# Forgetting heads: gate sums and split values in 4 KB runs, loads ordered a unit earlier, normalisation a unit later

## The chip, the cores and the metric

The kernel runs on one core of a Trainium2 chip. The metric is the device time of one execution in microseconds (us); before the change the median of three runs is 1835.76 us (1833.45 to 1837.6). The engines in the text are TensorE (PE; its weight loads are PEld), VectorE (DVE), ScalarE (ACT), GpSimd (POOL) and SyncE (SP). SP issues all DMAs of this kernel, in order, on one queue that 16 DMA engines serve.

## The reference: what is computed

One layer of a decoder trunk over 1024 tokens of width 1024, in float32. It has a SwiGLU feed-forward half-step, a token mixer of two groups of heads, and a second SwiGLU half-step, each with a residual, a LayerNorm and a modulation by a conditioning vector. The change touches the token mixer:

```
proj = h @ w_in                       # q_a k_a v_a (window heads), q_b k_b v_b (forgetting heads), f_logit
log_f = log_sigmoid(f_logit + b_forget)            # 1024 tokens x 8 heads
cum = cumsum(log_f, axis=tokens)                   # the gate sums
# window group: 8 heads of 64 on 2 key heads, 128-token window, ALiBi, a sink for each head
# forgetting group: 8 heads of 64, causal over all tokens
s[t, j] = q[t] . k[j] / 8 + cum[t] - cum[j]        # j <= t
o = softmax(s) @ v
out = concat(rms_norm(o_a) * gain_a, rms_norm(o_b) * gain_b) @ w_out
```

## The kernel before

All large products work on numbers split into a high and a low part (`split`, lines 101 to 103: ACT rounds to the high part, DVE subtracts to get the low one) and take three products for one (`mm3`), or two where the stacked operand holds both parts. The kernel is written with a tile framework. It takes the program's order as priority, places instructions on each engine by its own estimates of their times, gives a tile a place in its ring when one is free, and sets the waits. What an engine executes is therefore not the program's order exactly, but once placed, each engine and SP's queue go strictly in order. The rings (line 42) have 14 places of 8 KB a partition (h), four of 4 KB in each of z and q, and smaller ones; a ring's name is also a tile's name in the profile.

The token mixer runs from about 660 to 1170 us. First the values of all heads and the forget logits are computed for each of eight token blocks (lines 750 to 772). The high and low parts of the values, 64 + 64 columns a head, are stored to `vd`, whose order is head, token, column (line 763). The gate sums of 128 tokens by 64 (block, head) columns are made by two small products and a chain of small additions (lines 780 to 799), transposed, and stored to `cum_d`, whose order is block, head, token (line 805).

The 13 projections of queries and keys (`proj`) go to `qkd` in DRAM. They are cut into 26 halves that stand in a list of fillers: `fill` (line 925) adds a credit for each piece of attention work and runs the next filler when the credit covers it, and `due(n)` runs fillers until n projections are done. Behind the projections the list has the first half of the output projection.

The window heads come first (`swa_scores`, `swa_values`, `swa_finish` for two groups of eight blocks). Then come the forgetting heads, in four pairs `pr` of two heads `e`. Each head has two units, `q0` = 4 (query blocks 4 to 7) and `q0` = 0 (blocks 0 to 3), so there are 16 units. `fox_scores` (line 1060) makes for a unit four strips, from the last query block to the first: DVE adds the causal mask `cmask` to a 128x128 piece of the head's table `cb` of gate sums (line 1075), PE forms the scores, DVE adds the table to them and takes a running minimum (line 1092), ACT takes the exponential (line 1096). `fox_values` (line 1100) transposes the exponentials on PE, splits them, and multiplies by the split values. `mix` interleaves the values of unit k with the scores of unit k + 1.

`fox_init` (line 1050) issues a head's loads. It is called by strip 7 of the head's first unit. For the first head of a pair it loads the split values of both (`v_load`, h ring), and for each head the query stack, two key stacks, and the table `cb`: the 1024 gate sums of the head, copied to 128 partitions. These four are the z ring's four places for e = 0 and the q ring's for e = 1. `v_load` and the load of `cb` read eight runs of 512 B for each partition.

When a pair's four units are through, `fox_finish` (line 1130) takes the reciprocals of the denominators, transposes them, stores them to `rd` (`recip_rows`, line 863), and calls `normalise` (line 871). That loads them back, copied to 64 partitions for each head, multiplies the outputs, squares the result and adds it to `ssq` for the RMS norm: three DVE operations of 128x1024. The outputs are then stored to `ond`. `swa_finish` does the same with two pairs of a window group.

Of the kernel before, what the change touches and what calls it, by code (L numbers as in the profile page):

```python
# [7 lines left out]
F32 = mybir.dt.float32  # L8
F32R = mybir.dt.float32r
# [37 lines left out]
def layer_kernel(ctx, tc, xT, x, c, adaT, adab, wg1, wu1, wd1, wqk, wv1, wv2, bf, sinks,  # L47
# [29 lines left out]
    def dram(shape, name, dt=F32):  # L77
        return dr.tile(shape, dt, tag=name, name=name, bufs=1)
# [585 lines left out]
    def tok(t):  # L664
        return slice(t * P, (t + 1) * P)
# [61 lines left out]
              steps1)  # L727


    vd = dram([10, S, P], "vd")  # L730
    fz = const([P, NT, NH], "fz")

    def wv_load(src, ncol):
# [16 lines left out]
    for hf in range(2):  # L750
        for pz, (w, ncol) in enumerate(((wva, NV1), (wvb, NV2))):
            for k in range(4):
                t = hf * 4 + k
                p = psum("mm")
                for d in range(KD):
                    hi, lo = h2c(hf, d)
                    mm3(p[:, :ncol], hi[:, k * P:(k + 1) * P], lo[:, k * P:(k + 1) * P],
                        w[d][0], w[d][1], d == 0, d == KD - 1)
                vs = st("w", [P, 5, P], F32R)
                pv = p[:, :5 * HD].rearrange("p (h c) -> p h c", h=5)  # L760
                A.copy(vs[:, :, :HD], pv)
                V.tensor_tensor(vs[:, :, HD:], pv, vs[:, :, :HD].bitcast(F32), ALU.subtract)
                DMA.dma_start(vd[pz * 5:pz * 5 + 5, tok(t), :].rearrange("h t c -> t h c"), vs.bitcast(F32))
                if pz:
                    V.tensor_tensor(fz[:, t], p[:, 5 * HD:NV2], bfb, ALU.add)
                if hf == 0:
                    if t or pz:
                        steps[3 + t + 4 * pz]()
                    if t == 3 and pz:
                        steps[11]()  # L770
                else:
                    park_zn((xa, xb)[pz], pz, k, r1, xpark[0])
# [20 lines left out]
    pc = psum("tp")  # L793
    T.matmul(pc[:, :64], ones, flat(fl), start=True, stop=True)
    V.tensor_copy(flat(fz), pc[:, :64])
    for t in range(1, NT):
        V.tensor_tensor(fw[:, t], fw[:, t], fz[:, t - 1], ALU.add)
        if t + 1 < NT:
            V.tensor_tensor(fz[:, t], fz[:, t], fz[:, t - 1], ALU.add)
    pc = psum("tp")  # L800
    T.transpose(pc[:64, :P], flat(fw), ident)
    cum_sb = st("t", [64, P])
    A.copy(cum_sb, pc[:64, :P])
    cum_d = dram([NT, NH, P], "cum_d")
    DMA.dma_start(cum_d.rearrange("a b c -> (a b) c"), cum_sb)


# [44 lines left out]
        return r  # L852

    def v_load(h0):
        v = st("h", [P, NT, 2, P], F32R)
        for e in range(2):
            DMA.dma_start(v[:, :, e].bitcast(F32), vd[h0 + e].rearrange("(t p) c -> p t c", p=P))
        return v

    rd_d = [dram([n, NT, P], f"rd{i}") for i, n in enumerate((4, 4, 2, 2, 2, 2))]  # L860
# [148 lines left out]
    def swa_values(g, i):  # L1009
        d = swa[g]  # L1010
        sp = d["sp", i // 2][:, i % 2]
        if i == 0:
            d["on"] = st("h", [P, 2, S])
        on = d["on"]
        po = psum("o")
        js = [1] if i == 0 else [0, 1]
        for jj in js:
            pt = psum("tp")
            for hh in range(4):
                T.transpose(pt[:, tok(hh)], sp[:, hh, jj * P:(jj + 1) * P], ident)  # L1020
            ph, pl = st("t", [P, HT], F32R), st("t", [P, HT], F32R)
            split(ph, pl, pt)
            vt = va[:, i - 1 + jj, g]
            T.matmul(po, vt, ph, start=jj == js[0], stop=False)
            T.matmul(po, vt, pl, start=False, stop=jj == 1)
        t = st("t", [P, 2, P])
        pv = po.rearrange("p (b e c) -> p b e c", b=2, e=2)
        for e in range(2):
            own, oth = half_rows(e)
            A.copy(t[own], pv[oth, :, e])  # L1030
            V.tensor_tensor(on[own, :, tok(i)], pv[own, :, e], t[own], ALU.add)
        fill(1.6)

    def swa_finish(g):
        d = swa[g]
        mneg, den, on = d["mneg"], d["den"], d["on"]
        es = small([P, 4, NT], "es")
        for hh in range(4):
            A.activation(es[:, hh], mneg[:, hh], AF.Exp, bias=sinkb[:, 4 * g + hh:4 * g + hh + 1], scale=1.0)
        V.tensor_tensor(den, den, es, ALU.add)  # L1040
        recip_rows(flat(den), 4 * NT, rd_d[g])
        rt = st("h", [P, 2, S])
        for pp in range(2):
            normalise(on[:, pp], rd_d[g][2 * pp:2 * pp + 2], ssq_a, rt[:, pp])
            DMA.dma_start(ond[2 * g + pp], on[:, pp])


    fox = {}
# [1 line left out]
    def fox_init(pr, e):  # L1050
        ring = "zq"[e]
        if e == 0:
            fox[pr] = dict(vp=v_load(2 * pr), den=small([P, 2, NT], "den2"))
        d = fox[pr]
        d["qs", e] = q_stack(5 + pr, e, ring)
        d["ks", e] = k_stack(9 + pr, e, ring)
        cb = d["cb", e] = st(ring, [P, S])
        DMA.dma_start(cb.rearrange("p (a b) -> p a b", a=NT), cum_d[:, 2 * pr + e, :].partition_broadcast(P))

    def fox_scores(pr, e, q0):  # L1060
        def strip(i):
            if i == 7:
                fox_init(pr, e)
            d = fox[pr]
            if i == q0 + 3:
                if q0:
                    sa, sc = st("h", [P, 2, S]), st("h", [P, 2, S])
                    d["sp", e, q0] = {7: sa[:, 0], 6: sa[:, 1], 5: sc[:, 0], 4: sc[:, 1]}
                else:
                    sa = st("h", [P, 4, HT])  # L1070
                    d["sp", e, q0] = {k: sa[:, k] for k in range(4)}
            qs, ks, cb, den = d["qs", e], d["ks", e], d["cb", e], d["den"]


            V.tensor_tensor(cb[:, tok(i)], cb[:, tok(i)], cmask, ALU.add)
            L = (i + 1) * P
            if L <= 512:
                segs = [(0, L)]
            elif L == 640:
                segs = [(0, 384), (384, 256)]  # L1080
            else:
                segs = [(0, 512), (512, L - 512)]
            sp = d["sp", e, q0][i]
            m = None
            for k0, w in segs:
                pp = psum("mm")
                wm = max(w, 256)
                q = qs[:, tok(i)]
                T.matmul(pp[:, :wm], q, ks[0][:, k0:k0 + wm], start=True, stop=False)
                T.matmul(pp[:, :wm], q, ks[1][:, k0:k0 + wm], start=False, stop=True)  # L1090
                mn = small([P, 1], "mneg1", 8)
                V.tensor_tensor_reduce(sp[:, k0:k0 + w], pp[:, :w], cb[:, k0:k0 + w], scale=1.0,
                                       scalar=3e38 if m is None else m, op0=ALU.add, op1=ALU.min,
                                       accum_out=mn)
                m = mn
            A.activation(sp[:, :L], sp[:, :L], AF.Exp, bias=m, scale=-1.0, accum_out=den[:, e, i:i + 1])
            fill(L / 1200)
        return [lambda i=i: strip(i) for i in range(q0 + 3, q0 - 1, -1)]

    def fox_values(pr, e, q0):  # L1100
# [3 lines left out]
        def block(j):  # L1104
# [9 lines left out]
                T.transpose(pt[:, tok(i - q0)], sps[i][:, tok(j)], ident)  # L1114
            ph, pl = st("t", [P, HT], F32R), st("t", [P, HT], F32R)
            split(ph[:, c0:], pl[:, c0:], pt[:, c0:])
            vt = d["vp"][:, j, e]
            T.matmul(po[:, c0:], vt, ph[:, c0:], start=j == 0, stop=False)
            T.matmul(po[:, c0:], vt, pl[:, c0:], start=False, stop=j == q0 + 3)
            if j == q0 + 3:  # L1120
# [9 lines left out]
    def fox_finish(pr):  # L1130
        d = fox[pr]
        on, rt = d["on"][:, 0], d["on"][:, 1]
        recip_rows(flat(d["den"]), 2 * NT, rd_d[2 + pr])
        normalise(on, rd_d[2 + pr], ssq_b, rt)
        if pr < 3:
            DMA.dma_start(ond[4 + pr], on)

    def mix(a, b):

# [14 lines left out]
    for k, (g, i) in enumerate(units):  # L1154
        if k + 1 < len(units):
            if units[k + 1] == (1, 0):
                due(5)
            swa_scores(*units[k + 1])
        swa_values(g, i)
        if i == NT - 1:  # L1160
            swa_finish(g)
    ssq_b = st("b", [P, S])
    G.memset(ssq_b, 0.0)
    filler.append((0.0, lambda: out_init()))
# [4 lines left out]
    credit[0] = 0.0  # L1169
    units = [(pr, e, q0) for pr in range(4) for e in range(2) for q0 in (4, 0)]  # L1170
    due(7)
    for f in fox_scores(*units[0]):
        f()
    for k, u in enumerate(units):
        nxt = []
        if k + 1 < len(units):
            if units[k + 1][1:] == (0, 4):
                due(7 + 2 * units[k + 1][0])
            nxt = fox_scores(*units[k + 1])
        mix(fox_values(*u), nxt)  # L1180
        if u[1:] == (1, 0):
            fox_finish(u[0])
    on_last = fox[3]["on"][:, 0]
    while filler:
        filler.pop(0)[1]()
# [203 lines left out]
```

## Time and profile before

| what | value |
|---|---|
| time of the profiled execution | 1834.09 us |
| its span, first to last instruction | 1832.1 us |
| median of three runs (lowest, highest) | 1835.76 us (1833.45, 1837.6) |
| VectorE busy | 1546.1 us (84%) |
| ScalarE busy | 764.7 us (42%) |
| mean granted TensorE clock | 0.985 |
| moved by DMA | 303.44 MB, 166 GB/s over the span |

The span is the time from the first instruction to the last; the execution's own time has some 2 us around it. An engine's busy time over the span says how much room it has in the mean, and the windows view says it for a stretch. The granted clock is the share of full speed that TensorE was allowed.

### The profile page before, as it was taken

How to read it: one execution, taken by the hardware profiler on the slowest of the kernel's cores; microseconds unless marked ns; L12 is line 12 of the kernel's file. 1: busy time of each engine (PE TensorE's matmuls, PEld its weight loads, DVE VectorE, ACT ScalarE, POOL GpSimd, SP SyncE). 2: the span in 40 equal slices, each digit the busy share in tenths (PEclk: the TensorE clock that was granted, in tenths of full speed). 3: DMA queues.
4: the chain of work that ended last, by engine and by line, in shares of the span. 5: the costliest groups of instructions: out<-in, count | busy, mean ns of one | idle time of the engine just before them, and what ended most of it. 6: DMA issues, size and time to landing. Idle time of an engine off the chain costs nothing.

```text
span 1832.1 us, 23557 instructions
## 1 busy us (share of the span) xinstructions
PE 1755.3 (96%) x8114; PEld 1444.7 (79%) x8114; DVE 1546.1 (84%) x2805; ACT 764.7 (42%) x1465; POOL 23.0 (1%) x32
## 2 busy tenths in 40 slices
PE   7999999999999989999889899999999999999995
PEld 5788888888888879877667777778888888888884
DVE  7999999999597995378678797899788887878999
ACT  5432333233544442277356461543233333344480
POOL 0000000000000000000000000000000000000000
PEclk9999999999999999999989999999999999999998
DMA  9355555558754245855958863333223232675442
GB/s 360 127 197 178 193 193 193 170 173 290 233 167 143 86 134 180 242 148 154 229 143 198 215 205 107 138 109 128 97 99 131 88 108 92 223 231 166 133 144 80
DMA packets 163175, 303.44 MB, mean 166 GB/s; under 512 B 15384, under 2 KB 47728, under 8 KB 163056
## 3 DMA queue, kind: packets, MB, share of 16 engines
q1 hardware_dynamic: 163056, 301.94, 52.1%
q8 instruction: 64, 1.05, 0.2%
q14 instruction: 55, 0.45, 0.1%
HBM read 224.17 MB, written 77.71 MB: 165 GB/s over the span
## 4 chain that ended last, share of the span: by engine, by line
PE 73%; DVE 15%; DMA 6%; ACT 3%; issue 2%; SPq 0%; POOL 0%; DVEq 0%; ACTq 0%; POOLq 0%
PE y L106 10%; PE y L107 10%; PE y L108 10%; PE mm L106 9%; PE mm L108 9%; PE mm L107 9%; PE o L106 3%; PE o L108 3%; PE o L107 3%; DVE w L103 2%; DVE h L103 2%; DMA q<-cum_d 2%; PE tp L107 1%; PE tp L108 1%; PE tp L1114 1%
## 5 line engine op out<-in xcount | busy, mean ns | idle before, releaser
L102 ACT CAST w<-u 128x512 fp32r<-128x512 f32 x303 | 186.6, 622 | 393.1 <-PE y L108 160.2
L106 PE MATMUL y<-h,w 128*128 128x512 f32 x728 | 287.7, 395 | 5.0 <-ACT h L102 2.1
L107 PE MATMUL y<-h,w 128*128 128x512 f32 x728 | 285.6, 392 | 0.0
L108 PE MATMUL y<-h,w 128*128 128x512 f32 x728 | 285.2, 392 | 0.0
L103 DVE TENSOR_TENSOR w<-u,w 128x512 fp32r<-128x512 f32 x303 | 206.5, 686 | 23.4 <-ACT w L102 22.1
L106 PE MATMUL mm<-h,w 128*128 128x512 f32 x528 | 207.7, 394 | 18.7 <-ACT h L102 15.6
L107 PE MATMUL mm<-h,w 128*128 128x512 f32 x528 | 206.7, 392 | 0.3 <-DVE h L103 0.2
L108 PE MATMUL mm<-h,w 128*128 128x512 f32 x528 | 206.7, 392 | 0.0
L106 PEld LDWEIGHTS y<-h,w 128*128 128x128 f32 x728 | 137.5, 189 | 33.5 <-ACT h L102 2.5
L108 PEld LDWEIGHTS y<-h,w 128*128 128x128 f32 x728 | 137.0, 188 | 26.6
L107 PEld LDWEIGHTS y<-h,w 128*128 128x128 f32 x728 | 137.0, 188 | 26.3
L102 ACT CAST w<-t 128x512 fp32r<-128x512 f32 x106 | 65.5, 621 | 185.1 <-PE mm L108 70.3
L106 PEld LDWEIGHTS mm<-h,w 128*128 128x128 f32 x528 | 100.2, 190 | 40.9 <-ACT h L102 16.0
L107 PEld LDWEIGHTS mm<-h,w 128*128 128x128 f32 x528 | 100.0, 189 | 22.2 <-DVE h L103 1.5
L108 PEld LDWEIGHTS mm<-h,w 128*128 128x128 f32 x528 | 99.9, 189 | 21.3 <-DVE w L103 1.0
L102 ACT CAST z<-u 128x512 fp32r<-128x512 f32 x88 | 54.8, 623 | 105.2 <-PE y L108 46.8
L103 DVE TENSOR_TENSOR z<-u,z 128x512 fp32r<-128x512 f32 x88 | 60.5, 689 | 35.7 <-ACT z L102 35.6
L103 DVE TENSOR_TENSOR t<-tp,t 128x512 fp32r<-128x512 f32 (+1 forms) x126 | 72.8, 586 | 18.4 <-ACT t L102 17.7
L102 ACT CAST t<-tp 128x512 fp32r<-128x512 f32 (+1 forms) x126 | 61.8, 502 | 48.3 <-PE tp L1114 47.4
L102 ACT CAST w<-h 128x512 fp32r<-128x512 f32 x111 | 68.2, 617 | 29.4 <-PE o L108 10.5
L103 DVE TENSOR_TENSOR w<-h,w 128x512 fp32r<-128x512 f32 x111 | 75.6, 686 | 1.8 <-ACT w L102 1.8
L103 DVE TENSOR_TENSOR w<-t,w 128x512 fp32r<-128x512 f32 x106 | 72.8, 689 | 1.4 <-ACT w L102 0.8
(356 smaller groups left out, 3948.1 us busy)
## 6 DMA issues: line engine op xcount, KB each, us to landing
u<-aT SPq DMA_DIRECT2D x154, 256.0 KB, 2.7
q<-in_adaT SPq DMA_DIRECT2D x56, 512.0 KB, 3.4
u<-in_wg SPq DMA_DIRECT2D x92, 256.0 KB, 3.0
u<-in_wu SPq DMA_DIRECT2D x90, 256.0 KB, 2.8
aT<-z SPq DMA_DIRECT2D x44, 512.0 KB, 3.2
h<-in_wd SPq DMA_DIRECT2D x88, 256.0 KB, 4.5
qkd<-w SPq DMA_DIRECT2D x26, 512.0 KB, 4.1
aT<-b SPq DMA_DIRECT2D x22, 512.0 KB, 4.2
```

Source lines behind the costliest of these rows:

```text
L102: A.copy(hi, src)
L103: V.tensor_tensor(lo, src, hi.bitcast(F32), ALU.subtract)
L106: T.matmul(o, lh, rh, start=start, stop=False)
L107: T.matmul(o, lh, rl, start=False, stop=False)
L108: T.matmul(o, ll, rh, start=False, stop=stop)
L1114: T.transpose(pt[:, tok(i - q0)], sps[i][:, tok(j)], ident)
```

## The change

Four edits. `vd` is laid out as head, partition, block, column, so that a partition's eight blocks lie together, 4 KB, and the tile of values has the same order. The gate sums are brought into the order head, block before the transposition, by writing the additions to a tile `fo` with a stride, so that `cum_d` is head, block, token and a head's sums are one run of 4 KB. `fox_init` is taken out of strip 7 and called a unit ahead: for the first two heads before the first scores, for every other head at the start of the unit whose scores precede it; the table is loaded before the query stack; `v_load` stays in strip 7. And the loads and the three operations of `normalise`, with the store behind them, are put into a function that is run later: for a window group in block 2 of the next group, or after two strips of the next scores, and for a pair after two strips in the next unit. The last pair's is run after the loop.

```diff
-    vd = dram([10, S, P], "vd")
+    vd = dram([10, P, NT, P], "vd")
...
-                DMA.dma_start(vd[pz * 5:pz * 5 + 5, tok(t), :].rearrange("h t c -> t h c"), vs.bitcast(F32))
+                DMA.dma_start(vd[pz * 5:pz * 5 + 5, :, t, :].rearrange("h p c -> p h c"), vs.bitcast(F32))
...
+    fo = st("t", [P, NH, NT])
+    V.tensor_copy(fo[:, :, 0], fw[:, 0])
     for t in range(1, NT):
-        V.tensor_tensor(fw[:, t], fw[:, t], fz[:, t - 1], ALU.add)
+        V.tensor_tensor(fo[:, :, t], fw[:, t], fz[:, t - 1], ALU.add)
...
-    T.transpose(pc[:64, :P], flat(fw), ident)
+    T.transpose(pc[:64, :P], flat(fo), ident)
...
-    cum_d = dram([NT, NH, P], "cum_d")
+    cum_d = dram([NH, NT, P], "cum_d")
...
-        v = st("h", [P, NT, 2, P], F32R)
+        v = st("h", [P, 2, NT, P], F32R)
         for e in range(2):
-            DMA.dma_start(v[:, :, e].bitcast(F32), vd[h0 + e].rearrange("(t p) c -> p t c", p=P))
+            DMA.dma_start(v[:, e].bitcast(F32), vd[h0 + e])
...
+    later = []
+
     def swa_finish(g):
...
         recip_rows(flat(den), 4 * NT, rd_d[g])
-        rt = st("h", [P, 2, S])
-        for pp in range(2):
-            normalise(on[:, pp], rd_d[g][2 * pp:2 * pp + 2], ssq_a, rt[:, pp])
-            DMA.dma_start(ond[2 * g + pp], on[:, pp])
+
+        def rest():
+            rt = st("h", [P, 2, S])
+            for pp in range(2):
+                normalise(on[:, pp], rd_d[g][2 * pp:2 * pp + 2], ssq_a, rt[:, pp])
+                DMA.dma_start(ond[2 * g + pp], on[:, pp])
+        later.append(rest)
...
         if e == 0:
-            fox[pr] = dict(vp=v_load(2 * pr), den=small([P, 2, NT], "den2"))
+            fox[pr] = dict(den=small([P, 2, NT], "den2"))
         d = fox[pr]
-        d["qs", e] = q_stack(5 + pr, e, ring)
         d["ks", e] = k_stack(9 + pr, e, ring)
         cb = d["cb", e] = st(ring, [P, S])
-        DMA.dma_start(cb.rearrange("p (a b) -> p a b", a=NT), cum_d[:, 2 * pr + e, :].partition_broadcast(P))
+        DMA.dma_start(cb, cum_d[2 * pr + e].rearrange("a b -> (a b)").partition_broadcast(P))
+        d["qs", e] = q_stack(5 + pr, e, ring)
...
         def strip(i):
-            if i == 7:
-                fox_init(pr, e)
             d = fox[pr]
+            if i == 7 and e == 0:
+                d["vp"] = v_load(2 * pr)
...
     def fox_finish(pr):
...
         recip_rows(flat(d["den"]), 2 * NT, rd_d[2 + pr])
-        normalise(on, rd_d[2 + pr], ssq_b, rt)
-        if pr < 3:
-            DMA.dma_start(ond[4 + pr], on)
+
+        def rest():
+            normalise(on, rd_d[2 + pr], ssq_b, rt)
+            if pr < 3:
+                DMA.dma_start(ond[4 + pr], on)
+        later.append(rest)
...
         if i == NT - 1:
             swa_finish(g)
+        elif i == 2:
+            run_all(later)
+            later.clear()
...
     due(7)
+    fox_init(0, 0)
+    fox_init(0, 1)
     for f in fox_scores(*units[0]):
         f()
     for k, u in enumerate(units):
         nxt = []
+        if k and k + 2 < len(units) and units[k + 2][2]:
+            if not units[k + 2][1]:
+                due(7 + 2 * units[k + 2][0])
+            fox_init(*units[k + 2][:2])
         if k + 1 < len(units):
-            if units[k + 1][1:] == (0, 4):
-                due(7 + 2 * units[k + 1][0])
             nxt = fox_scores(*units[k + 1])
+        if later:
+            nxt.insert(2, later.pop())
         mix(fox_values(*u), nxt)
         if u[1:] == (1, 0):
             fox_finish(u[0])
+    run_all(later)
```

## Rows read from the trace of the kernel before

**Rows 1.** The page: busy time of PE; the chain that ended last, by engine.
```profile
PE   1755.3 (96%) x8114; PEld 1444.7 (79%) x8114; DVE 1546.1 (84%) x2805; ACT 764.7 (42%) x1465; POOL 23.0 (1%) x32
PE 73%; DVE 15%; DMA 6%; ACT 3%; issue 2%; SPq 0%; POOL 0%; DVEq 0%; ACTq 0%; POOLq 0%
```

**Rows 2.** Windows: stretch, its us, busy us of each engine, PE's clock, DMA share, GB/s.
```profile
862.00:1040.00 178.00, 157.93 (x796) 126.45 (x795) 129.39 (x326) 93.41 (x208) 2.56 (x1) 0.95 0.75 191
1040.00:1100.00 60.00, 59.25 (x317) 47.13 (x317) 53.53 (x133) 36.87 (x87) 0.00 (x0) 0.98 0.69 207
902.00:905.40 3.40, 3.40 (x14) 2.82 (x13) 2.15 (x7) 1.31 (x4) 0.00 (x0) 0.50 1.05 260
946.40:956.60 10.20, 6.01 (x19) 4.84 (x20) 4.94 (x12) 2.17 (x6) 0.00 (x0) 0.50 0.71 168
...
1038.50:1041.90 3.40, 3.40 (x12) 2.69 (x11) 2.84 (x11) 1.79 (x5) 0.00 (x0) 0.51 1.16 272
```

**Rows 3.** Timeline of DVE: start, us, instruction, in brackets the idle time before it.
```profile
873.93 0.29 DVE L1075 TENSOR_TENSOR z<-z,cmask 128x128 f32<-128x128 f32 x1 [6.05 <-DMA z<-cum_d]
899.92 0.29 DVE L1075 TENSOR_TENSOR q<-q,cmask 128x128 f32<-128x128 f32 x1 [3.65 <-DMA q<-cum_d]
949.64 0.29 DVE L1075 TENSOR_TENSOR q<-q,cmask 128x128 f32<-128x128 f32 x1 [6.62 <-DMA q<-cum_d]
...
965.73 0.68 DVE L1092 CUSTOM_DVE_ANT_0 h<-mm,q 128x512 f32<-128x512 f32 x1
...
977.82 0.29 DVE L1075 TENSOR_TENSOR z<-z,cmask 128x128 f32<-128x128 f32 x1 [1.50 <-DMA z<-cum_d]
997.67 0.29 DVE L1075 TENSOR_TENSOR q<-q,cmask 128x128 f32<-128x128 f32 x1 [3.09 <-DMA q<-cum_d]
1035.97 0.29 DVE L1075 TENSOR_TENSOR z<-z,cmask 128x128 f32<-128x128 f32 x1 [4.80 <-DMA z<-cum_d]
```

**Rows 4.** Timeline of PE: four instructions that ended its longer idle times.
```profile
882.17 0.45 PE L1089 MATMUL mm<-z,z 128*128 128x384 f32 x1 [2.00 <-DVE s_mneg L1092]
901.18 0.50 PE L1089 MATMUL mm<-q,q 128*128 128x512 f32 x1 [3.40 <-DVE s_mneg L1092]
950.59 0.79 PE L1119 MATMUL o<-t,h 128*128 128x512 f32 x1 [6.36 <-DVE t L103]
1036.93 0.39 PE L1089 MATMUL mm<-q,q 128*128 128x256 f32 x1 [3.77 <-DVE s_mneg L1092]
```

**Rows 5.** Timeline of PE and SP near 897; SP's longest waits, 862 to 1040.
```profile
896.76 0.28 PE L1090 MATMUL mm<-z,z 128*128 128x256 f32 x1
...
896.95 0.45 SPq L841 DMA_DIRECT2D z<-qkd  x1
...
SPq L869 <- ACT s_row L868: 18.3, 3, 9.1
```

**Rows 6.** DMA: line 1058's landings; issues, KB of each, median us to landing.
```profile
DMA to landing us min/median/max: 9.0/10.2/10.5
...
h<-in_adaT SPq DMA_DIRECT2D x16, 512.0 KB, 8.5
...
vd<-w SPq DMA_DIRECT2D x16, 320.0 KB, 2.6
h<-vd SPq DMA_DIRECT2D x10, 512.0 KB, 7.2
...
b<-gate_row SPq DMA_DIRECT2D x3, 512.0 KB, 6.8
```

**Rows 7.** Normalisation: DVE's wait, line 875's operations, line 873's landings.
```profile
DVE h L875 <- DMA h<-rd: 2.1, 1, 2.1
...
L875 DVE TENSOR_TENSOR h<-h x4: 1215/1221/1226, 955.3 to 1108.4; 128x1024 f32<-128x1024 f32 x4
...
DMA to landing us min/median/max: 3.6/4.5/11.8
```

More of the change, by code (lines that the diff above doesn't have):

```diff
@@ L1022, in swa_values @@
             split(ph, pl, pt)
-            vt = va[:, i - 1 + jj, g]
+            vt = va[:, g, i - 1 + jj]
             T.matmul(po, vt, ph, start=jj == js[0], stop=False)
@@ L1116, in block @@
             split(ph[:, c0:], pl[:, c0:], pt[:, c0:])
-            vt = d["vp"][:, j, e]
+            vt = d["vp"][:, e, j]
             T.matmul(po[:, c0:], vt, ph[:, c0:], start=j == 0, stop=False)
```

## The prediction

> **What bounds the kernel now.** I read first the page's busy table and chain of waits: TensorE (PE) is busy for 1755.3 of 1832.1 us and holds most of the chain [rows 1], so a change is worth only what it gives PE: idle time, or time at the low clock. The windows view over the stage that the change touches comes next [rows 2]. Of the 178 us from 862 to 1040, in which nearly three of the four pairs of forgetting heads run, PE is idle for 178 - 157.9 = 20.1 us, and its granted clock is 0.95. In the 60 us behind it the same work runs with 0.75 us of idle, while VectorE (DVE) is busy for 53.5 of 60 us: without stalls the stage is PE's, and DVE has just room.
>
> The time-ordered list of DVE shows where the idle time comes from [rows 3]. Six of the eight heads begin with a `cmask` addition (line 1075, strip 7) that finds its table of gate sums (`cb`, loaded from `cum_d`) not landed: 6.05 + 3.65 + 6.62 + 1.50 + 3.09 + 4.80 = 25.7 us. DVE takes its instructions in order, so what stands behind that addition waits too, though it belongs to another unit: the first score reduction of the head whose mask waited until 949.64 starts at 965.73. The addition is put into DVE's order some 16 us before anybody needs it, as soon as the scheduler believes the table to be there. PE then runs out of operands: 3.40, 6.36 and 3.77 us behind three of these waits [rows 4]. Each of the three is followed, or overlapped, by a stretch at clock 0.50 or 0.51, half of full speed (1.2 in place of 2.4 GHz): 902.0 to 905.4, 946.4 to 956.6 and 1038.5 to 1041.9 [rows 2]. PE was busy there for 3.40, 6.01 and 3.40 us; at full clock the same work takes half, so the low clock costs 1.7 + 3.0 + 1.7 = 6.4 us. The other waits (0,0 at 6.05, and 1.50 and 3.09) I price at nothing on PE; under the first one PE had projections to do. Together the masks cost PE 13.5 us idle and 6.4 us slow, 19.9 us.
>
> **The change part by part.** *The order "a unit ahead".* It changes where the loads stand in the program. When they start is another matter: the loads of head (1,0) begin at 896.95, 0.2 us behind the start of the last product on the tiles whose places they take (896.76) [rows 5]. They already go out when a place in the z or q ring comes free, and each head needs all four places of its ring. The new position can't free a place earlier. I take 0 us; at best it saves the time that the table stands behind other issues of SyncE (SP): SP waits 18.3 us in three pieces, at most 9.1 us, for the reciprocal rows (line 869) [rows 5], a wait that the change keeps. At worst it loses nothing by itself, since no head's ring is shared with the unit that is running. `due` forces no projection earlier either: by the credit arithmetic of `fill` the projections that it asks for are done one unit before, in both versions. The table now goes ahead of `qs`; that is two issues of SP, under 1 us of its own.
>
> *Runs of 4 KB.* The table of a head (512 KB: one 4 KB row copied to 128 partitions) is now read as eight runs of 512 B for each partition, and lands 10.2 us after issue (9.0 to 10.5) [rows 6]. Afterwards it is one run of 4 KB for each partition. The trace has a load of just that form: the gate row, 512 KB, one 4 KB row to 128 partitions, median 6.8 us [rows 6]. The bounds: 8.5 us, the slow end among 512 KB loads in 4 KB runs (`adaT`, beside other loads), and 6.8 us. I take 6.8, the same form, so 3.4 us earlier. If DVE comes to each mask when it does now, the waits become 6.05 - 3.4 = 2.65, 0.25, 3.22, 0, 0 and 1.40 us: 7.5 in place of 25.7. On PE the 3.40 goes, 6.36 becomes 3.0 and 3.77 becomes 0.4: 10.1 us less idle. Of the slow stretches I keep one of 3.4 us behind the 3.0 (the idle of 3.40 was followed by one such), 1.7 us, so 4.7 of the 6.4 come back. Sum: -14.8 us. Next late behind the masks are then DVE's ordinary steps, which the stretch 1040 to 1100 shows to be hidden [rows 2].
>
> The Trainium skill, page "DMA: Bandwidth & Descriptors", speaks against this term: its Specifications give 512 B as the least transfer for line rate, and its section "Why small descriptors are slow (HBM only)" counts a fixed 3 cycles for each packet beside one for every 32 B. By that, eight runs of 512 B cost 8 x 19 = 152 cycles against 131 for one of 4 KB, and the table would land after an estimated 10.2 x 131 / 152 = 8.8 us. The gate row's 6.8 us against the table's 10.2 [rows 6] doesn't agree with so small a step, though the two were not loaded beside the same traffic.
>
> *The split values.* Their loads (512 KB in 512 B runs, 7.2 us now) get 4 KB runs too, their stores (2.6 us) keep 512 B runs that then lie 4 KB apart [rows 6]. No stall of the stage falls on either: values are used a unit after the load. Bounds: the loads gain up to 7.2 - 6.8 = 0.4 us by the gate row, or lose 1.3 by the 8.5; the stores could double to 5.2 us, which is what the first window product would come later if nothing lay between. Projections do, so I take 0.
>
> *The gate sums' order.* One more copy of 128x8 and seven additions that write with a stride. A mask addition of 128x128 takes 0.29 us [rows 3], which bounds the copy from above; a stride that doubled the seven would cost 7 x 0.29 = 2.0 at most. I take 0.3 us, on DVE, with PE on projections beside it; it counts in full here.
>
> *The normalisation put off.* Each finish has three operations of 1.22 us on DVE [rows 7], 3.7 us a pair (7.3 for the two pairs of a window group). They are moved by about half a unit, not removed; the reciprocals, their transpose and the write to `rd` stay. What it can gain: the wait of 2.1 us for `h<-rd` [rows 7], and with it the 2.00 us of PE at 882.17 [rows 4]. What it can lose is the last rival's price. It is also one more tile held in the h ring for half a unit. I take 0, between -2.0 and that rival.
>
> Sum: -14.8 + 0.3 = -14.5. The profiled execution took 1834.09 us (1832.1 of span and 2.0 around it), the median of the runs is 1835.76, the lowest 1833.45. 1834.1 - 14.5 = 1819.6; I say **1819.5**.
>
> **Rivals.**
> *All stalls go.* If the schedule gives the tables enough lead, the whole 20.1 us of idle and the 6.4 us of low clock come back: 1834.1 - 26.5 = 1807.6. For it: heads (1,0) and (3,1) have no wait today. Against: the mask is placed by an expected landing, not by need, in all six others.
>
> *The run length is worth half.* A copy of one 4 KB row to 128 partitions may be held back by its source rather than by its runs. With a landing of 8.5 us (1.7 earlier) the waits of 3.65, 6.62 and 4.80 shrink by 1.7 each, PE gets 3 x 1.7 = 5.1 us, and the idle left (1.7, 4.7, 2.1) keeps most of the slow stretches: about 1 us back. 1834.1 - 6.1 = 1828. The skill's estimate of 8.8 us is near this case and would give 1829. For it: the value loads, with the same 512 B runs but no copying, land in 7.2 us. Against: the gate row's 6.8.
>
> *The wait moves along.* If the scheduler's own estimate of the load shrinks with the runs, it puts the mask additions 3.4 us earlier, and DVE meets them as early as now. The six waits stay, 1834. This is also the case in which the change doesn't do what it says. For it: the mask stands 16 us ahead of its use [rows 3]. Against: the waits differ from 0 to 6.6 us, so that arrival is only loosely tied to the estimate.
>
> *The normalisation becomes the wait (slower).* The rows of reciprocals are copied to 64 partitions by two loads behind the write of `rd`. They land 4.5 us after issue as a rule, 11.8 us when a table is loaded beside them [rows 7]. Put off into the middle of the next unit, they stand on SP behind the seven issues of a head's load and share the engines with its 2 MB (four tiles of 512 KB). Then DVE waits 11.8 - 4.5 = 7.3 us at line 875, four times in the stage (window group 1, pairs 0 to 2), with strips and splits queued behind it: 29 us. The mask waits cost PE 19.9 / 25.7 = 0.77 us for each us of DVE, so 22.6 us: 1834.1 - 14.5 + 22.6 = 1842. It decides against the change from 14.5 / 0.77 = 19 us of such waits. Against: today's total is 2.1 us, and half a unit is given for the landing: nearly three pairs of four units each in 178 us make a unit some 15 us, its half 7.
>
> **How the numbers follow.** Forecast 0.52 (1809 to 1825), all gone 0.11 (about 1808), half 0.13 (1825 to 1831), wait moves along 0.12 (1830 to 1838), normalisation 0.12 (1836 to 1848). From the rivals on both sides the range is 1804 to 1836: it leaves out the slower rival and a little beyond the best. The measurement of this kernel tells 0.2%, 3.7 us, from no change. Faster: 0.52 + 0.11 + 0.12 of the half = 0.75; same: 0.01 of the half, 0.10 of the moved wait and 0.02 of the last = 0.13; slower: the other 0.02 of the moved wait and 0.10 of the last = 0.12.
>
> **What would show it.** Right: loads of `cum_d` that land in about 7 us; the waits of line 1075 at 5 to 10 us in total; PE idle about 10 us over the stage, with one or two half-clock stretches; first loads of each head still right behind the last product on its ring. Wrong: landings above 8.5 us; waits of line 1075 unchanged although landings fell (the wait moved along); a new wait of line 875 for `rd` above 10 us; or PE idle in the value products behind a late load of `vd`.

## The result, and the profile after

The changed kernel takes 1817.76 us (median of 4 runs, 1817.26 to 1819.38) against 1834.62 us for the kernel before (4 runs): a ratio of 0.9907 [0.989, 0.9924], 0.9% faster. The forecast was 1819.5, in a range of 1804 to 1836. The profiled span fell from 1832.1 to 1815.5 us, by 16.6 us. That is the sum of a larger gain than forecast and of a loss that was not forecast, and the two can be read apart.

The page of the changed kernel, its busy PE and its chain of waits by engine:

```profile
PE   1750.9 (96%) x8114; PEld 1439.7 (79%) x8114; DVE 1547.4 (85%) x2806; ACT 764.8 (42%) x1465; POOL 23.0 (1%) x32
PE 83%; DVE 10%; ACT 3%; DMA 2%; issue 1%; POOL 0%; SPq 0%; DVEq 0%; ACTq 0%; POOLq 0%
```

Against [rows 1], DMA falls from 6 to 2% of the chain and DVE from 15 to 10%, and PE takes their place.

The windows of the changed kernel, with the columns of [rows 2]: the stage, the 40 us near its end, and a stretch within those.

```profile
862.00:1040.00 178.00, 174.13 (x913) 138.04 (x912) 148.85 (x381) 108.65 (x248) 2.61 (x1) 1.00 0.75 213
1060.00:1100.00 40.00, 35.68 (x167) 28.18 (x165) 31.27 (x54) 16.30 (x34) 0.00 (x0) 0.91 0.67 219
1076.60:1083.40 6.80, 5.86 (x13) 4.14 (x14) 5.43 (x9) 3.51 (x6) 0.00 (x0) 0.50 0.92 268
```

PE's idle time in these 178 us, which now hold more of the work, fell from 20.1 [rows 2] to 178 - 174.13 = 3.9 us, and its granted clock rose from 0.95 to 1.00: no half-clock stretch is left there. Behind the stage there is a new one, 6.8 us at 0.50.

DVE's time-ordered list of the changed kernel, for one head whose mask had waited 6.62 us [rows 3] and for the last mask of all:

```profile
937.11 0.29 DVE L1082 TENSOR_TENSOR q<-q,cmask 128x128 f32<-128x128 f32 x1
945.99 0.68 DVE L1099 CUSTOM_DVE_ANT_0 h<-mm,q 128x512 f32<-128x512 f32 x1
...
1065.61 0.28 DVE L1082 TENSOR_TENSOR q<-q,cmask 128x128 f32<-128x128 f32 x1
```

The same list of the kernel before, for the last mask:

```profile
1088.53 0.28 DVE L1075 TENSOR_TENSOR q<-q,cmask 128x128 f32<-128x128 f32 x1
```

No mask addition has an idle time in brackets any more: the 25.7 us of waits are gone, all of them. The last mask is a landmark for the end of the stage. It moved from 1088.53 to 1065.61, so the stage gained 22.9 us; the last value product, which moved from 1096.04 to 1072.94, says nearly the same, 23.1. From there to the end of the span it is 1832.1 - 1088.5 = 743.6 us before and 1815.5 - 1065.6 = 749.9 after: behind the stage the changed kernel gives back 6.3 us. 22.9 - 6.3 is the 16.6.

The windows from 862 to the last mask, before and after, hold nearly the same work (1052 and 1043 products):

```profile
862.00:1088.53 226.53, 205.72 (x1052) 164.50 (x1051) 173.67 (x439) 123.82 (x279) 2.56 (x1) 0.95 0.73 191
862.00:1065.61 203.61, 198.78 (x1043) 157.53 (x1042) 173.05 (x436) 123.78 (x281) 2.61 (x1) 1.00 0.72 206
```

PE's idle time falls from 20.8 to 4.8 us, by 16.0, and its busy time by 6.9 us, at a clock of 1.00 in place of 0.95: together the 22.9.

What is given back stands in the time-ordered lists of the changed kernel. PE's, an output product:

```profile
1077.54 0.79 PE L106 MATMUL y<-w,h 128*128 128x512 f32 x1 [4.21 <-ACT w L102]
```

DVE's, the scaling of an output weight:

```profile
1076.09 0.75 DVE L914 SCALAR_TENSOR_TENSOR u<-u,gaincol,b 128x512 f32<-128x512 f32 x1 [1.53 <-DMA u<-in_wout]
```

SP's, a late reload of the residual and the fourth second-half output weight:

```profile
1070.78 0.43 SPq L1215 DMA_DIRECT2D h<-xpark  x1
1071.26 0.43 SPq L913 DMA_DIRECT2D u<-in_wout  x1
```

Read backwards: PE waits 4.21 us for a weight that ACT splits, ACT waits for DVE's scaling, DVE for the raw weight, and SP issues its load only at 1071.26, behind the reloads of the residual. The idle time and the half clock behind it are the loss.

The loads of the changed kernel's tables (line 1064): the four on the z ring (ns of one issue; first and last start), and the landings of all eight:

```profile
L1064 SPq DMA_DIRECT2D z<-cum_d x4: 577/932/1315, 863.2 to 1005.1; - x4
...
DMA to landing us min/median/max: 5.7/7.3/9.0
```

The median of 10.2 us [rows 6] became 7.3.

### The profile page after: what moved, and what is told of

Its sections match the earlier page's. It is cut to its first block, busy times and chain, and to the rows that moved or that the text cites. A ratio compares the mean times of both kernels' runs of the same rounds, so it can differ in the third digit from the quotient of the medians.

```text
span 1815.5 us, 23554 instructions
## 1 busy us (share of the span) xinstructions
PE 1750.9 (96%) x8114; PEld 1439.7 (79%) x8114; DVE 1547.4 (85%) x2806; ACT 764.8 (42%) x1465; POOL 23.0 (1%) x32
## 4 chain that ended last, share of the span: by engine, by line
PE 83%; DVE 10%; ACT 3%; DMA 2%; issue 1%; POOL 0%; SPq 0%; DVEq 0%; ACTq 0%; POOLq 0%
PE y L106 11%; PE y L107 11%; PE y L108 11%; PE mm L108 10%; PE mm L106 10%; PE mm L107 9%; PE o L106 3%; PE o L108 3%; PE o L107 3%; PE tp L108 2%; PE tp L107 2%; PE tp L106 2%; DVE h L103 1%; PE tp L1121 1%; PE o L1125 1%
## 5 line engine op out<-in xcount | busy, mean ns | idle before, releaser
L107 PEld LDWEIGHTS y<-h,w 128*128 128x128 f32 x728 | 136.9, 188 | 25.9 <-DVE h L103 0.2
L103 DVE TENSOR_TENSOR t<-tp,t 128x512 fp32r<-128x512 f32 (+1 forms) x126 | 73.0, 586 | 20.8 <-ACT t L102 19.5
L102 ACT CAST w<-h 128x512 fp32r<-128x512 f32 x111 | 68.1, 616 | 28.8 <-PE o L108 10.5
```

Of the source, the lines that this page charges most:

```text
L102: A.copy(hi, src)
L103: V.tensor_tensor(lo, src, hi.bitcast(F32), ALU.subtract)
L107: T.matmul(o, lh, rl, start=False, stop=False)
```

## The experiments

The theory was that of the prediction: one 4 KB run for each partition lands the table sooner, so the mask that DVE meets too early no longer stops it; the order, the values' layout and the put-off normalisation are worth nothing. The rivals were the order (loads truly earlier) and the put-off normalisation as a gain. Ratios are to the kernel before, with their 95% intervals.

**The gate sums' layout alone.**

```diff
+    fo = st("t", [P, NH, NT])
+    V.tensor_copy(fo[:, :, 0], fw[:, 0])
...
-    cum_d = dram([NT, NH, P], "cum_d")
+    cum_d = dram([NH, NT, P], "cum_d")
...
-        DMA.dma_start(cb.rearrange("p (a b) -> p a b", a=NT), cum_d[:, 2 * pr + e, :].partition_broadcast(P))
+        DMA.dma_start(cb, cum_d[2 * pr + e].rearrange("a b -> (a b)").partition_broadcast(P))
```

> Only the gate sums' edit: the order head, block, token in DRAM, so that a head's table is loaded in 4 KB runs; loads, normalisation and values stay as before. Theory A (run length: the table lands earlier, the early mask addition waits less): landings of the table fall from 10.2 us to about 7, the waits of the mask additions from 25.7 us in total to 5 to 10, and the time by 12 to 17 us, ratio 0.991 to 0.9935. Rival B (the order a unit ahead does it): landings may fall, waits of over 15 us stay, ratio 0.997 to 1.0. Rival C (the normalisation put off does it): as B.

1808.37 us, 0.9866 [0.9853, 0.9879]: this part alone brings 1.3%, more than the whole change and more than the 0.991 to 0.9935 that was expected of it. DVE's list of this kernel, the only two mask waits left and the last mask:

```profile
868.32 0.29 DVE L1077 TENSOR_TENSOR z<-z,cmask 128x128 f32<-128x128 f32 x1 [1.52 <-DMA z<-cum_d]
935.18 0.29 DVE L1077 TENSOR_TENSOR q<-q,cmask 128x128 f32<-128x128 f32 x1 [0.30 <-DMA q<-cum_d]
...
1065.79 0.28 DVE L1077 TENSOR_TENSOR q<-q,cmask 128x128 f32<-128x128 f32 x1
```

SP's list of this kernel (line 852 loads the head's keys, 871 writes the reciprocal rows, 1060 is the table, 913 an output weight):

```profile
920.85 2.69 SPq L852 DMA_DIRECT2D q<-qkd  x4
930.56 0.33 SPq L871 DMA_DIRECT2D rd<-s_row  x1
930.99 0.37 SPq L1060 DMA_DIRECT2D q<-cum_d  x1
...
1033.61 0.43 SPq L913 DMA_DIRECT2D u<-in_wout  x1
...
1037.24 3.81 SPq L913 DMA_DIRECT2D u<-in_wout  x3
```

The landings of its tables:

```profile
DMA to landing us min/median/max: 4.2/6.3/7.6
```

And SP's list of the kernel before, for the same head:

```profile
928.97 2.69 SPq L850 DMA_DIRECT2D q<-qkd  x4
938.69 0.33 SPq L869 DMA_DIRECT2D rd<-s_row  x1
939.12 0.37 SPq L1058 DMA_DIRECT2D q<-cum_d  x1
```

The two kernels issue in the same order, so only the landing differs. Before, the mask ran 949.64 - 939.12 = 10.5 us after its issue, having waited 6.62 [rows 3]: DVE had come to it 3.9 us after issue. Here it ran 935.18 - 930.99 = 4.2 us after, having waited 0.30: DVE again came 3.9 us after issue, and the table was there. That is the theory on one head, and it excludes "the wait moves along". Behind the stage nothing is lost: from 1065.8 to the end of the span (1809.4) it is 743.6 us, as before, and SP issued the four second-half output weights between 1033.6 and 1041.1, ahead of the reloads of the residual.

**The order alone** (init a unit ahead, table ahead of the queries, values in the strip; old layouts).

```diff
         d["ks", e] = k_stack(9 + pr, e, ring)
         cb = d["cb", e] = st(ring, [P, S])
...
+        d["qs", e] = q_stack(5 + pr, e, ring)
...
+        if k and k + 2 < len(units) and units[k + 2][2]:
...
+            fox_init(*units[k + 2][:2])
```

> Only the order: loads of a head issued a unit ahead in the program, the table ahead of the query stack, the value loads left in strip 7; both layouts in DRAM as before, normalisation as before. Theory A: the loads start when a ring place comes free, as before, the table still lands after about 10 us, and the mask additions still wait 15 to 26 us in total: ratio 0.997 to 1.001. Rival B: waits below 8 us although landings stay at 10 us, ratio 0.990 to 0.994.

1826.43 us, 0.996 [0.9948, 0.9972]. SP's list of this kernel (line 1057 is the table):

```profile
923.21 2.37 SPq L850 DMA_DIRECT2D q<-qkd  x4
925.62 0.59 SPq L1057 DMA_DIRECT2D q<-cum_d  x1
...
941.94 0.88 SPq L869 DMA_DIRECT2D rd<-s_row  x1
```

Who waited for its tables (total us, times), and the landings:

```profile
  DVE q L1075: 12.7, 3
  DVE z L1075: 1.2, 1
...
DMA to landing us min/median/max: 9.8/10.9/11.3
```

The landing is as slow as ever, but the waits are 13.9 us in place of 25.7; 15 to 26 us and 0.997 to 1.001 were expected, so theory A missed, though rival B's 8 us was not reached either. Head by head, the one in the list has its table issued ahead of SP's wait on line 869 and no longer behind it, and its mask waits 1.07 us in place of 6.62. The first head's table goes out at 855.90 in place of 863.07, and its wait of 6.05 us is gone. The second head's wait grows from 3.65 to 9.13. The other three waits fall together from 9.4 to 3.7. The last mask runs at about 1074.3, 14.2 us earlier, and then 1824.7 - 1074.3 = 750.4 us follow, 6.8 more than before. The late weight is here too, PE's list:

```profile
1085.80 1.22 PE L106 MATMUL y<-w,h 128*128 128x512 f32 x2 [3.72 <-ACT w L102]
```

**The normalisation put off, alone.**

```diff
-        normalise(on, rd_d[2 + pr], ssq_b, rt)
+        def rest():
+            normalise(on, rd_d[2 + pr], ssq_b, rt)
...
+        later.append(rest)
```

> Only the normalisation put off (window groups and pairs). Theory A: the mask waits stay above 20 us; the 2.0 us of TensorE behind the first normalisation may go: ratio 0.998 to 1.003. Rival C: mask waits below 10 us because the write and read of the reciprocal rows no longer stand ahead of the tables on SyncE: ratio 0.990 to 0.995. Rival D (it becomes a wait): waits for the reciprocal rows at line 877 or so above 10 us and ratio above 1.003.

1836.68 us, 1.002 [1.0011, 1.0029]: slightly slower. Mask waits are 16.8 + 9.1 = 25.9 us with landings of 10.3 us, as before. The wait of 2.1 us for `rd` [rows 7] is gone; one of 0.7 us stands at the last pair.

**The mask held back.** No part of the change; the strip-7 mask addition of every head but the first is ordered on DVE behind the last score reduction of the unit before.

```diff
+            if i == 7 and last:
+                with tc.issue_after(last[0]):
+                    V.tensor_tensor(cb[:, tok(i)], cb[:, tok(i)], cmask, ALU.add)
```

> Nothing of the change. The first mask addition of each head but the first (strip 7) is ordered on VectorE behind the last score reduction of the unit before, so it is no longer placed ahead of need; the loads keep their 512 B runs. Theory A (VectorE stands in order behind a mask addition that nobody needs yet): landings stay at 10.2 us, the mask waits fall from 25.7 to about 6 (head 0,0 alone, which is not ordered), and nearly all of the 19.9 us of TensorE come back: ratio 0.989 to 0.992. Rival E (the tables are really late): the same waits stand at the ordered place, ratio 0.998 to 1.002.

1825.0 us, 0.9961 [0.9948, 0.9973]; 0.989 to 0.992 was expected. DVE's list of this kernel, its two mask waits (the first is the head left unordered):

```profile
871.99 0.29 DVE L1080 TENSOR_TENSOR z<-z,cmask 128x128 f32<-128x128 f32 x1 [5.30 <-DMA z<-cum_d]
973.33 0.29 DVE L1078 TENSOR_TENSOR z<-z,cmask 128x128 f32<-128x128 f32 x1 [3.71 <-DMA z<-cum_d]
```

The landings of its tables:

```profile
DMA to landing us min/median/max: 8.6/9.7/10.9
```

With the old layout and slow landings, moving the instruction on DVE takes the waits from 25.7 to 9.0 us and the last mask to 1070.3, 18.2 us earlier. So it was the place in DVE's order, together with the landing, that cost the time. One head is no clean case of it: the schedule moved too, and the table that had stood behind SP's wait on line 869 is issued at 925.58 here, ahead of it. And the 3.71 us left at the ordered place are a table that is truly late, as rival E has it. The time missed because 751.0 us follow the last mask, 7.4 more than before. This kernel has late output weights as well, though it hasn't the order. SP's list, the third and fourth second-half weight behind the reloads of the residual, and PE's, the first wait for one:

```profile
1075.95 0.43 SPq L911 DMA_DIRECT2D u<-in_wout  x1
1078.66 0.43 SPq L911 DMA_DIRECT2D u<-in_wout  x1
...
1082.17 0.73 PE L106 MATMUL y<-w,h 128*128 128x512 f32 x2 [0.99 <-ACT w L102]
```

How much of the 7.4 us they cost was not isolated.

**The late weight: a place of its own.** The changed kernel, with the raw second-half output weights in one tile of the h ring.

```diff
+                raw = st("h", [P, 4, HT]) if n else None
-                ws.extend(out_w(k, n) for k in range(4))
+                ws.extend(out_w(k, n, raw[:, k] if n else None) for k in range(4))
```

> The changed kernel, and beside it one thing: the four raw output weights of the second half (n = 1) are loaded into one tile of the h ring instead of four places of the u ring, so that they need not wait for the u ring's places. Theory T (behind the heads' stage the change loses what the gate sums' edit alone doesn't: the fourth weight is loaded at 1071 us, behind sixteen reloads of the residual, and TensorE idles 4.2 us and then runs 6.8 us at half clock): that wait goes, ratio 0.985 to 0.988, within 0.1% of the gate sums' edit alone (0.9866). Rival U (the difference lies elsewhere): ratio stays at 0.990 to 0.992.

1819.89 us, 0.993 [0.9916, 0.9945]. PE's list of this kernel:

```profile
1075.65 0.80 PE L106 MATMUL y<-w,h 128*128 128x512 f32 x1 [4.60 <-ACT w L102]
```

SP's list, the first of the four loads (the other three follow at 1072.22):

```profile
1068.98 0.37 SPq L913 DMA_DIRECT2D h<-in_wout  x1
```

The expectation failed: the loads still stand behind the reloads of the residual on SP's queue, the first one 0.1 us behind the end of the last of these (issued at 1068.44 in 0.43 us), and the wait stays; 0.993 lies beyond the rival's 0.990 to 0.992 too. It doesn't tell whether the place in the u ring was the cause.

**The gate sums' layout with each other part.** The edit of the first experiment, and on top of it the order, the values' layout, or the put-off normalisation (diffs as above; the values' is the one below).

```diff
-    vd = dram([10, S, P], "vd")
+    vd = dram([10, P, NT, P], "vd")
...
-            DMA.dma_start(v[:, :, e].bitcast(F32), vd[h0 + e].rearrange("(t p) c -> p t c", p=P))
+            DMA.dma_start(v[:, e].bitcast(F32), vd[h0 + e])
```

> Gate sums in 4 KB runs and the loads ordered a unit ahead; values and normalisation as before. Theory T (both edits remove the same waits of the mask additions, and the order makes the late output weight): no mask waits, last mask addition near 1066 us as with the gate sums' edit alone, but the late output weight is back, ratio 0.989 to 0.991. Rival V (the two add up): ratio below 0.985. Rival W (the order costs nothing, the loss comes from the normalisation or the values): ratio 0.986 to 0.987.

> Gate sums and split values in 4 KB runs; order of loads and normalisation as before. Theory T: nobody waits for the values, 0 +- 0.1% against the gate sums' edit alone, ratio 0.9855 to 0.988. Rival W: ratio 0.989 or more.

> Gate sums in 4 KB runs and the normalisation put off; values and order of loads as before. Theory T: 0 to +0.2% against the gate sums' edit alone (alone it cost 0.2%), ratio 0.9865 to 0.989. Rival W: ratio above 0.989.

With the order: 1817.06 us, 0.9913 [0.9898, 0.9927], slower than the layout alone and level with the whole change, at the upper edge of theory T's 0.989 to 0.991. One mask wait of 3.7 us is left, where none was expected. The last mask stands at 1064.3, 1.5 us earlier than without the order, and the late weight is back on PE's list:

```profile
1075.91 0.80 PE L106 MATMUL y<-w,h 128*128 128x512 f32 x1 [3.92 <-ACT w L102]
```

With the values' layout: 1809.45 us, 0.9872 [0.9857, 0.9888], no difference; their loads land after 6.4 us in the median (6.0 without the edit), their stores after 2.6 in both. With the put-off normalisation: 1813.3 us, 0.989 [0.9872, 0.9908], 0.24% above the layout alone as against 0.2% above the kernel before when alone; the interval overlaps that of the layout alone, so it is the two results together that speak for a small loss.

**How long a run must be.** The gate sums as runs of 1 KB and of 2 KB (one run each, for the landing).

```diff
-    cum_d = dram([NT, NH, P], "cum_d")
+    cum_d = dram([4, NH, 2 * P], "cum_d")
...
-        DMA.dma_start(cb.rearrange("p (a b) -> p a b", a=NT), cum_d[:, 2 * pr + e, :].partition_broadcast(P))
+        DMA.dma_start(cb.rearrange("p (a b) -> p a b", a=4), cum_d[:, 2 * pr + e, :].partition_broadcast(P))
```

> Only the size of the runs: the gate sums lie in DRAM with two blocks of a head together, so a table is read in four runs of 1 KB for each partition; all else as before. Theory A (the landing is set by the number of runs, 1024 packets of 512 B against 128 of 4 KB): 10.2 us falls to 7 to 9 us, mask waits between 5 and 15 us, time near 1815 to 1825 us. Rival (the copying of one row is what is slow, or line rate is reached at 512 B): landing above 9.5 us, time above 1825.

> As with 1 KB, with two runs of 2 KB for each partition. Theory A: landing 6 to 7.5 us, mask waits 1 to 8 us, time 1806 to 1818 us. Rival: landing above 9 us.

The waits (total us, times) and landings of the 1 KB kernel:

```profile
  DVE q L1077: 11.8, 3
  DVE z L1077: 11.0, 3
...
DMA to landing us min/median/max: 8.8/9.6/10.6
```

The same of the 2 KB kernel:

```profile
  DVE z L1077: 4.1, 2
  DVE q L1077: 2.5, 1
...
DMA to landing us min/median/max: 5.9/6.7/8.2
```

The 1 KB expectation (7 to 9 us) missed: 9.6 us is hardly less than the 10.2 of 512 B, and landing and time are those of the rival (above 9.5 us, above 1825). At 2 KB theory A's figures hold. The gain lies between 1 and 2 KB: 10.2, 9.6, 6.7, 6.3 us for runs of 512 B, 1, 2 and 4 KB. So the landing isn't proportional to the number of runs either: halving it from 1024 to 512 a table gains 0.6 us, from 512 to 256 gains 2.9, and from 256 to 128 gains 0.4. Waits follow the landing, 25.7, 22.8, 6.6 and 1.8 us, and so do the times: 1832.26 (before, beside these two), 1825.93, 1814.17, and 1808.37 from the first experiment.

The Trainium skill, page "DMA: Bandwidth & Descriptors", section "Why small descriptors are slow (HBM only)", would by its fixed cost for each packet give estimates of 9.4, 9.0 and 8.8 us for 1, 2 and 4 KB, from the 10.2 of 512 B. The 1 KB landing agrees with it; 6.7 and 6.3 do not, and the measurement decides.

**The late weight: more output units earlier.** The changed kernel, and the gate sums' layout alone as control, with the ratio that charges the cheap units of the filler raised, so that more of them go beside the heads.

```diff
-RATIO2 = 0.3
+RATIO2 = 0.5
```

> The changed kernel with one constant changed: RATIO2 0.5 in place of 0.3, so that by the credit arithmetic six instead of four units of the first output half stand inside the loop over the heads. Theory T (the changed kernel loses behind the stage because a late unit of the first half holds places of the u and w rings that the weights of the second half need): the 4.2 us wait and the half-clock stretch at 1077 us go, ratio 0.985 to 0.989. Rival U (these fillers are not it): wait stays, ratio 0.990 to 0.993.

> Control for the last: the gate sums' edit alone with RATIO2 0.5. Theory T: there is no late weight to remove, so 0 +- 0.15% against the gate sums' edit alone, ratio 0.985 to 0.988. Rival X (more output units inside the loop are worth something, or cost something, by themselves): below 0.985 or above 0.989.

The windows view of the changed kernel with this edit:

```profile
1060.00:1100.00 40.00, 39.01 (x190) 30.46 (x189) 35.75 (x63) 17.06 (x35) 2.02 (x1) 1.00 0.68 220
```

PE's idle time in these 40 us falls from 4.3 to 1.0 us and the clock is 1.00: the late weight is cured. The time, 1812.12 us, 0.9899 [0.9884, 0.9915], is 5.6 us under the changed kernel's, near the 6.3 lost; but it stands just outside the 0.985 to 0.989 expected, and its interval overlaps that of the changed kernel, taken on another occasion. The control, 1809.6 us, 0.9884 [0.9867, 0.99], taken beside it and just above its 0.985 to 0.988, shows no gain where no weight is late; the two are 2.5 us apart, against 9.4 between the changed kernel and the layout alone. No version run is clearly faster than the gate sums' layout alone.

## Why the prediction was right, and where not

**The main term: mechanism right, size too small.** Its steps (a sooner landing, DVE no longer held at a mask it meets too early, PE's idle time and low clock back) are shown by the gate sums' layout alone and, from the other side, by the mask held back. But -14.8 was mis-sized; the stage gained 22.9 us. Up to the last mask, PE's idle time fell by 16.0 us where I had 10.1, and its busy time by 6.9, where I had 4.7 from the clock. I had also counted one half-clock stretch too few. Before, the windows and PE's list have a fourth, 1.7 us by the same working, behind an idle time that I did not list:

```profile
1014.70:1018.10 3.40, 3.40 (x11) 2.86 (x12) 2.98 (x10) 2.09 (x7) 0.00 (x0) 0.51 0.92 229
...
1014.53 0.60 PE L1119 MATMUL o<-t,h 128*128 128x384 f32 x1 [2.54 <-DVE t L103]
```

No mask stands right before it, and in the layout alone it is still there: 2.54 us idle up to 996.21, then a clock of 0.50 from 996 to 1000. In the whole change 1.34 us of idle are left of it, at 997.67, and the clock stays at 1.00.

The median landing alone doesn't explain the larger gain: 7.3 us in the changed kernel is no better than the 6.8 I took. My error was one landing for all heads. With the layout alone they range from 4.2 to 7.6 us, and the head that I left waiting 3.22 us had the 4.2; with the whole change a table may also go out earlier, the second one at 872.2 against 888.4 before. The 2.00 us at 882.17 [rows 4] that I left standing are gone too, as are 0.99 and 0.42 us of PE behind two of the waits that I priced at nothing (at 978.76 and 999.34).

**The order: 0 us was wrong both ways.** Alone it gains 0.4%. For one head that is the very thing I had called its best case: the table no longer stands behind SP's wait on line 869 [rows 5], and 5.6 us of wait go. But 6.05 us go at the first head, whose table is issued 7.2 us earlier, though I had taken the loads to go out already when a place comes free. Beside the sooner landing this gain has nothing left to save, for both work on the same 25.7 us. And it has a price that I had not looked for, since I read no further than the stage: the weight that is late at 1077. "At worst it loses nothing by itself" is the step that failed. In all four kernels with the order (the whole change, the order alone, the layout with the order, and the output weights in the h ring) PE waits 3.7 to 4.6 us there, unless the filler's ratio is raised; with the layout alone it does not. The order is not the only way to it, since the kernel with the mask held back has late weights without it. What goes with it is the last first-half output unit: its closing DVE operation (line 925 of the changed kernel) starts 17 us ahead of the last value product in the kernel before, in the layout alone and in the changed kernel with the raised ratio, none of which has the wait, 7 us ahead of it in the changed kernel, in the order alone and in the layout with the order, and 2 us ahead with the mask held back. Why the schedule leaves that unit later (1065.8 against 1056.3 in the layout alone), and the weight's load with it, was only argued and stays open.

**The small terms.** The values' layout at 0 is right. The gate sums' extra order at +0.3 us can't be seen apart. The normalisation at 0, between -2.0 and its rival, is about right: the wait for `rd` fell from 2.1 to 0.5 us, but with the layout alone it is gone altogether, so that this gain isn't the normalisation's; and alone the normalisation costs 0.2%, for a reason that no run here isolates.

**The rivals.** "All stalls go" (1807.6) comes nearest for the stage, and for the layout alone, 1808.4, in the time as well; not for its reason, since there SP issues the tables in the same order as before. "The run length is worth half" is near what 1 KB would have brought: 1825.9 by one run. "The wait moves along" and "the normalisation becomes the wait" did not happen.

So 1819.5 came within 2 us of 1817.76 because two errors of opposite sign, some 8 us too little gain and 6.3 us of unforeseen loss, nearly cancel. That closeness is luck.

## What to carry to other kernels

An instruction that an in-order engine meets before its load has landed stops everything behind it, whoever that belongs to; look for it where small operations carry idle time, and shorten the load, issue it ahead of foreign waits on its queue, or put the instruction later. Two cures of one stall need not add up: time each part alone, since here one layout edit of a few lines beat the change that contains it. And follow a moved load to the end of the program, not to the end of its stage.

## What had not been expected of the hardware

A 512 KB load that copies one 4 KB row to 128 partitions lands in about 10 us with runs of 512 B or 1 KB and in about 6.5 with 2 or 4 KB (medians of the eight tables in one trace each; 7.3 in the changed kernel, with its other order of loads); the step lies between 1 and 2 KB. In the changed kernel PE's idle time of 4.21 us, which ended at 1077.54, was followed by work at a granted clock of 0.50 up to 1083.4: PE was busy there for 5.86 us, which takes half of that at full clock, so the low clock cost 2.9 us beside the 4.2.
